# Two more tiles of u sent to DRAM, with the adding transfers of the last four tiles issued inside the down projection, and the first half's closing additions written to SBUF

## The chip, the cores and the metric

One Trainium2 chip, one core of it. The metric is the device time of one execution in microseconds, the median of three runs; lower is better. A profiled execution gives, beside its own time, a span: from the start of the first recorded instruction to the end of the last.

## The reference

One decoder layer over 256 tokens with 2048 channels: a normalised input projection, two kinds of attention, an output projection with a residual, and then the part that matters here:

```python
h = _rmsnorm(x, norm_mlp_pre[layer])
u = jnp.square(jax.nn.relu(h @ w_up[layer]))        # 256 x 8192
x = x + _rmsnorm(u @ w_down[layer], norm_mlp_post[layer])
```

Everything is float32, and the weights (w_up 2048 x 8192, w_down 8192 x 2048) come from DRAM once per run.

## The kernel before

**Split products.** Each float32 operand is split in two parts: `hi` is the value rounded by a ScalarE copy to the short format that TensorE takes at full speed, `lo = value - hi` is made by VectorE (L307, L308). A product is then three matmuls, hi.hi, lo.hi and hi.lo (`three`, `mm` at L297). So each weight tile of 128 x 1024 costs a load into a buffer `raw` on SP's DMA queue, a `hi` on ScalarE and a `lo` on VectorE, before TensorE uses it for twelve matmuls (two token blocks, two column halves, three parts). There are five `raw` buffers and eight `hi`/`lo` pairs; the class `Weights` makes the tiles six ahead of their use.

**Steps of seven products.** Some steps ("w" in the lists of steps) take two weight tiles and two column halves together by a scheme of seven products in place of eight (`seven_products`, L1055). Their two weight tiles are loaded as one pair of 1 MB on POOL's queue (L375), into one of two buffers in turn (`ab_down` and `c` in the first half of the down projection, `ab_down` and `u01` in the second). VectorE forms sums of them (L362, L366, L367), which are then split like other weights, and sums of the tokens' blocks (`four_sums`, L1011 to L1013), which are split into `s`. Three of the seven products go to banks of their own (`md`), and `close` (L1071) combines these into four tiles `c` in SBUF, which are added to the four accumulators at the end of the half.

**Up and down.** The up projection runs over eight column chunks j of 1024. Each is evacuated by `up_evac` (L934): ScalarE takes the relu into a buffer `r` (two of them), TensorE transposes it (L301), and ScalarE squares it into a tile of u. There are 16 such tiles g, each 128 x 1024 for 512 of the 8192 channels: chunk j gives tiles 2j and 2j + 1. The down projection has two halves c of 1024 output columns. Each half goes through all 16 tiles of u; a step takes 128 channels ("k") or 256 ("w"), so there are four k or two w to a tile. The steps of seven are those of `DOWN_SEVEN`: 5, 7, 9, 11, 15, 17, 19, 21, 25, 27, 29 in the first half (step kp uses tile kp // 2), and the odd ones from 3 to 27 in the second. The four accumulators `y` of the first half take four banks of PSUM, those of the second the other four; the second half's `md` take the banks of the first half's `y`.

**The parts of u.** In each half `split_u` makes uhi and ulo of the next tile while the present one is used. For tiles g in `AWAY` (4 to 11) ulo is not made by VectorE: after `up_evac`, `lo_away` (L954) lets ScalarE write the negated rounded tile into `r` (L961), stores that in DRAM (`ukeep`, L963, on ScalarE's queue), and later a transfer on POOL's queue adds u to it there (L968, `accum_op`), two halves of 256 KB each. What is then in DRAM is u - uhi. ulo is loaded back from it on POOL's queue (`load_lo`, L997) in both halves. For other tiles VectorE makes ulo in the first half, and `keep_u` (L1001, SP's queue) stores it for the second.

**What sets the order.** The instructions of each engine, and of each DMA queue, run in the order in which the program issues them. That order is made by a planner (`Flow`): side tasks are generators that yield planned microseconds, TensorE's instructions move the planned clock on (0.216 us a matmul), and after each group of matmuls `pump` lets every task whose time has come issue its next instructions. `until` and `finish` issue a task's instructions at once up to a point. `lo_away` yields 34 us (48 us for tiles 10 and 11) between the stores and the adding transfers. POOL's queue holds the pair loads, the u loads, the loads of kept sums (`skeep`) and the adding transfers. A transfer that waits for its buffer holds up all behind it on its queue.

**The first half's closing.** `half_evac` (L1207) runs as a task at the start of the second half. For each of the four accumulators VectorE adds `more` (the tile `c`) in PSUM (L1216), ScalarE squares the sum from PSUM and sums it over the row (L1164), and VectorE multiplies it by the gain into SBUF (L1211), one accumulator late. At the first step of seven of the second half (kp = 3, after six k steps) `flow.finish(h_evac)` (L1259) issues what is left of it before the banks become `md`.

Of the kernel before, what the change touches and what calls it, by code (L numbers as in the profile page):

```python
# [22 lines left out]
AF = mybir.ActivationFunctionType  # L23
OP = mybir.AluOpType
# [5 lines left out]
NB = S // P  # L30
# [84 lines left out]


DOWN_SEVEN = ((5, 7, 9, 11, 15, 17, 19, 21, 25, 27, 29), range(3, 28, 2))
AWAY = range(4, 12)
SHARED = [k for k in DOWN_SEVEN[0] if k in DOWN_SEVEN[1]]
GT = FF // 512  # L120
DOWN_STEPS = [[s for kp in range(2 * GT)
# [143 lines left out]
def layer(nc, tc, io):  # L265
# [688 lines left out]
    def lo_away(g):  # L954

        ukeep[g] = dram.tile([P, CW], F32, name=f"ukeep{g}")
        u = uT[g].rearrange("p k s -> p (k s)")
        for h in range(2):
            c = slice(h * 512, (h + 1) * 512)
            t = late["up"].tile([P, 512], F32, tag="r", bufs=2, name=f"neg{g}_{h}")  # L960
            nc.scalar.activation(t.bitcast(F32R), u[:, c], AF.Copy, scale=-1.0)  # L961
            yield 1.0
            nc.scalar.dma_start(out=ukeep[g][:, c], in_=t)  # L963
            yield 7.0
        yield 34.0 if g < 10 else 48.0
        for h in range(2):
            c = slice(h * 512, (h + 1) * 512)
            nc.gpsimd.dma_start(out=ukeep[g][:, c], in_=u[:, c], accum_op=OP.add)  # L968
            yield 2.0

    def split_u(c, g):
        if (c, g) == (0, 0):
# [186 lines left out]

        return uT[i + n // 2].rearrange("p k s -> p (k s)")[:, (n % 2) * 512:(n % 2) * 512 + 512]  # L1160

    def square(n, b):
        junk = dpl["dp"].tile([P, 512], BF16, tag="junk", bufs=1, name=f"junkd{n}{b}")
        nc.scalar.activation(junk, y[b][n], AF.Square, accum_out=ssd[b][:, n:n + 1])  # L1164

    def gain(n, b):
        yg[n, b] = spare(2 * b, n)
# [38 lines left out]

    def half_evac(more, g_half):  # L1207

        def half_gain(b, n):
            yg[n, b] = more[b, n]  # L1210
            nc.vector.tensor_tensor(out=more[b, n], in0=y[b][n], in1=g_half[n], op=OP.mult)  # L1211

        done = []
        for n in range(2):
            for b in range(NB):
                nc.vector.tensor_tensor(out=y[b][n], in0=y[b][n], in1=more[b, n], op=OP.add)  # L1216
                square(n, b)
                yield 1.0
                if done:
                    half_gain(*done.pop())  # L1220
                    yield 1.0
                done.append((b, n))
        half_gain(*done.pop())

    def three_more(out, a, w):

# [10 lines left out]
    for c in range(2):  # L1237

        for i, (b, n) in enumerate(PARTS):
            y[b][2 * c + n] = bank(4 * c + i, f"y{b}{2 * c + n}")  # L1240
        accs = {(b, n): y[b][2 * c + n] for b, n in PARTS}
        ws = DOWN_SEVEN[c]
        for t, (what, k, tiles) in enumerate(wide_d[c]):
            g = (2 * k if what == "w" else k) // 4
            u = us[c, g]
            if g >= GT - 2 and c:
                break
            if what == "k":
                w = weights.get(tiles[0])
                for b, n in PARTS:  # L1250
                    down_mm(c, u, k, b, n, w, t == 0, t == len(wide_d[c]) - 1)
                    flow.pump()
                weights.free(tiles[0])
            else:
                if k == ws[0]:
                    if not c:
                        flow.finish(*u_last)
                    else:
                        flow.finish(h_evac)  # L1259
                    m = {i: bank(4 * (1 - c) + o, f"md{i}_{c}") for o, i in enumerate((1, 6, 7, 5))}  # L1260
                blocks = [[tok(u[x], 2 * (k % 2) + kk, bb) for x in range(2)] for kk, bb in ((0, 0), (1, 0), (1, 1))]
                seven_products(tiles, (blocks, left.pop((c, k))), accs, m, k == ws[0], k == ws[-1])
                if k == ws[-1]:
                    more = close([spare(10, i) for i in range(4)] if c else closing(), m)
                if not c and k in SHARED:
                    keep_s(k)
            while c and loaded[0] < min(g + (2 if g > 2 else 1), GT - 1):
                loaded[0] += 1
                load_lo(c, loaded[0])
            nxt = (c, g + 1) if g < GT - 1 else (1, 0)  # L1270
            if nxt not in us:
                if not c and g > 1 and g - 1 not in AWAY:
                    keep_u(g - 1)
                us[nxt] = split_u(*nxt)
            if (c, what, k) == (0, "k", 3):
                weights.limit += 1
            if (c, what, k) == (0, "k", 36):
                g_half = [late["up"].tile([P, 512], F32, tag="r", bufs=2, name=f"g_half{n}") for n in range(2)]
                for n in range(2):
                    load_gain(n, g_half[n])  # L1280
            if (c, what, k) == (1, "k", 40):
                flow.start(x_back())
                for n in (2, 3):
                    load_gain(n, spare(4, n))
        if not c:
            keep_u(GT - 1)
            h_evac = flow.start(half_evac(more, g_half))
# [64 lines left out]
```

## Time and profile before

| | |
|---|---|
| median of 3 runs | 1050.45 us (1049.29 to 1050.63) |
| the profiled execution's own time | 1050.77 us |
| its span | 1049.0 us |
| TensorE busy | 1035.0 us (99%) |
| VectorE busy | 841.1 us (80%) |
| ScalarE busy | 639.5 us (61%) |
| POOL busy | 74.0 us (7%) |
| mean granted clock of TensorE | 0.997 |
| up projection, last chunk, first matmul of the down projection | from 659.2 us, 704.5 us |
| first and second half of the down projection meet at | about 873 us |

How the rows of a profile are read: a timeline row has the start, the duration, the engine (PE is TensorE, PEld its weight load, DVE VectorE, ACT ScalarE, SP and POOL the others; a q behind the name is the engine's queue), the line, the operation, what it writes and reads (out<-in), the shape and types, the count of merged instructions, and in brackets the idle time before it and what ended that. A row of waits has who waited for whom, the total, the count and the longest. A row of DMA issues has out<-in, the queue, the count, the size and the median time from issue to landing; a row of DMA queues has packets, MB and the time of its packets as a share of all 16 DMA engines. Matmuls overlap in the array: one is recorded with 0.39 us, and the next starts 0.227 us after it.

### The profile page before, as it was taken

To read this page: it belongs to the slowest core of one execution; us is meant where nothing else is said; L and a number is where in the kernel's file an instruction comes from. 1 tells how busy PE (TensorE), PEld (TensorE's weight loads), DVE (VectorE), ACT (ScalarE), POOL (GpSimd) and SP (SyncE) were. 2 spreads that over 40 slices of the span, in tenths; PEclk is the share of its full clock that TensorE was granted. 3 is DMA by queue.
4 is the path that set the end of the run, shared out by engine and by line. 5 is a ranking of instruction groups with operands and counts; after the bars stand their busy time and mean duration, and the time that the engine had idled before them with its cause. 6 is when DMAs were issued, how large, how long until landed. Compare 5 with 4: busy or idle time off the path is not lost.

```text
span 1049.0 us, 13419 instructions
## 1 busy us (share of the span) xinstructions
PE 1035.0 (99%) x4828; PEld 860.1 (82%) x4828; DVE 841.1 (80%) x1129; ACT 639.5 (61%) x870; POOL 74.0 (7%) x113
## 2 busy tenths in 40 slices
PE   9999999999999999999999999999999999999996
PEld 6888889888888788888888888788888888788885
DVE  6676536567557669999999999798989987998895
ACT  6584436565545466565766767666757564766561
POOL 0000000000000000000010102000101001112100
PEclk9999999999999999999999999999999999999998
DMA  9975447454447295646769769479696968789862
GB/s 299 357 236 153 139 133 238 145 162 157 145 160 240 82 369 188 208 155 213 234 201 299 191 221 265 154 263 342 207 379 224 356 213 290 264 307 352 331 232 81
DMA packets 85363, 240.87 MB, mean 230 GB/s; under 512 B 7472, under 2 KB 12080, under 8 KB 84912
## 3 DMA queue, kind: packets, MB, share of 16 engines
q1 hardware_dynamic: 62992, 165.70, 46.6%
q0 software_dynamic: 19568, 69.74, 20.3%
q10 hardware_dynamic: 2736, 4.57, 1.3%
q8 instruction: 38, 0.62, 0.2%
q14 instruction: 29, 0.24, 0.1%
HBM read 218.49 MB, written 21.50 MB: 229 GB/s over the span
## 4 chain that ended last, share of the span: by engine, by line
PE 87%; DVE 7%; issue 2%; DMA 2%; ACT 1%; SPq 0%; POOL 0%; DVEq 0%; POOLq 0%; ACTq 0%
PE acc_u L297 21%; PE y L297 20%; PE acc_o L297 8%; PE m L297 6%; PE md L297 5%; PE acc_v L297 4%; PE acc_qk L297 4%; DVE lo L308 3%; PE acc_ckv L297 2%; PE acc_ukv L297 2%; PE acc_q L297 2%; PE acc_cq L297 2%; PE acc_k L297 2%; PE acc_uq L297 2%; PE rt L301 1%
## 5 line engine op out<-in xcount | busy, mean ns | idle before, releaser
L308 DVE TENSOR_TENSOR lo<-raw,hi 128x1024 fp32r<-128x1024 f32 (+3 forms) x207 | 233.7, 1149 | 80.7 <-ACT hi L307 80.0
L307 ACT ACTIVATE hi<-raw 128x1024 fp32r<-128x1024 f32 (+3 forms) x207 | 203.6, 997 | 76.1 <-DMA raw<-in_w_in 15.3
L297 PE MATMUL acc_u<-hi,hT_hi 128*128 128x512 f32 x356 | 141.7, 398 | 0.0
L297 PE MATMUL acc_u<-hi,hT_lo 128*128 128x512 f32 x356 | 139.1, 391 | 0.4 <-DVE hT_lo L308 0.4
L297 PE MATMUL acc_u<-lo,hT_hi 128*128 128x512 f32 x356 | 138.7, 390 | 0.0
L297 PE MATMUL y<-lo,uhi 128*128 128x512 f32 x352 | 137.1, 389 | 1.0 <-DVE lo L308 1.0
L297 PE MATMUL y<-hi,uhi 128*128 128x512 f32 x352 | 137.3, 390 | 0.0
L297 PE MATMUL y<-hi,ulo 128*128 128x512 f32 x352 | 137.0, 389 | 0.0
L312 DVE SCALAR_TENSOR_TENSOR lo<-raw,gcol,hi 128x1024 fp32r<-128x1024 f32 x74 | 92.5, 1280 | 11.4 <-ACT hi L311 11.3
L311 ACT ACTIVATE hi<-raw,gcol 128x1024 fp32r<-128x1024 f32 x74 | 83.2, 1148 | 28.7 <-DMA raw<-in_w_up 16.0
L297 PEld LDWEIGHTS acc_u<-hi,hT_lo 128*128 128x128 f32 x356 | 66.8, 188 | 15.1 <-DVE hT_lo L308 0.9
L297 PEld LDWEIGHTS y<-lo,uhi 128*128 128x128 f32 x352 | 66.1, 188 | 15.0 <-DVE lo L308 1.4
L297 PEld LDWEIGHTS acc_u<-lo,hT_hi 128*128 128x128 f32 x356 | 67.0, 188 | 12.9
L297 PEld LDWEIGHTS y<-hi,ulo 128*128 128x128 f32 x352 | 66.1, 188 | 13.8
L297 PEld LDWEIGHTS acc_u<-hi,hT_hi 128*128 128x128 f32 x356 | 66.9, 188 | 12.7
L297 PEld LDWEIGHTS y<-hi,uhi 128*128 128x128 f32 x352 | 66.1, 188 | 13.6
L307 ACT ACTIVATE hi<-u 128x1024 fp32r<-128x1024 f32 (+1 forms) x38 | 37.4, 991 | 42.2 <-DVE u L367 30.1
L308 DVE TENSOR_TENSOR lo<-st_down,hi 128x1024 fp32r<-128x1024 f32 x48 | 57.6, 1220 | 4.2 <-ACT hi L307 4.2
L307 ACT ACTIVATE hi<-st_down 128x1024 fp32r<-128x1024 f32 x48 | 49.9, 1051 | 5.7 <-DVE st_down L367 3.2
L297 PE MATMUL md<-hi,s 128*128 128x512 f32 x144 | 52.2, 390 | 0.8 <-ACT uhi L980 0.8
L297 PE MATMUL acc_o<-hi,mixT_hi 128*128 128x512 f32 x128 | 51.8, 405 | 0.0
L297 PE MATMUL acc_o<-hi,mixT_lo 128*128 128x512 f32 x128 | 50.2, 392 | 0.0
(332 smaller groups left out, 2150.2 us busy)
## 6 DMA issues: line engine op xcount, KB each, us to landing
raw<-in_w_down SPq DMA_DIRECT2D x80, 512.0 KB, 5.8
raw<-in_w_up SPq DMA_DIRECT2D x76, 512.0 KB, 4.9
raw<-in_w_in SPq DMA_DIRECT2D x55, 512.0 KB, 5.0
ab<-in_w_up POOLq DMA_DIRECT2D x22, 1024.0 KB, 5.6
raw<-in_w_out SPq DMA_DIRECT2D x32, 512.0 KB, 4.3
ab_down<-in_w_down POOLq DMA_DIRECT2D x13, 1024.0 KB, 8.8
ulo<-ukeep POOLq DMA_DIRECT2D x23, 512.0 KB, 7.1
u<-in_w_down POOLq DMA_DIRECT2D x6, 1024.0 KB, 8.8
```

The source lines that it names most:

```text
L297: nc.tensor.matmul(out, a, b, start=start, stop=stop)
L301: nc.tensor.transpose(out, a, ident)
L307: nc.scalar.activation(hi, src, AF.Copy)
L308: nc.vector.tensor_tensor(out=lo, in0=src, in1=hi.bitcast(F32), op=OP.subtract)
L311: nc.scalar.activation(hi, src, AF.Copy, scale=g)
L312: nc.vector.scalar_tensor_tensor(out=lo, in0=src, scalar=g, in1=hi.bitcast(F32), op0=OP.mult, op1=OP.subtract)
```

## The change

Three things, all after the sixth up chunk:

- `AWAY` grows by the tiles 12 and 13. Each of them now has its negated rounded tile stored from ScalarE during the last up chunk, its u added in DRAM, and its ulo loaded on POOL's queue in the first half. VectorE's subtraction for it in the first half and the store of its ulo on SP go.
- For tiles 10 to 13 (`g >= LATE`) the adding transfers wait, in the planner, for the start of the down projection (`dpl` filled), and are then issued 4, 9, 24 and 29 planned us later, the second half of a tile 10 planned us after the first. Before, those of 10 and 11 were issued 48 planned us after their stores.
- `half_evac` first adds all four accumulators and `more` into SBUF (into `more` itself), which frees the banks; 20 planned us later it squares and multiplies each from SBUF, one each 5 planned us. The second half's `md` banks are taken when the four additions are issued (`added`), not when the whole task is.

```diff
-AWAY = range(4, 12)
+AWAY = range(4, 14)
+LATE = 10
...
@@ lo_away
-        yield 34.0 if g < 10 else 48.0
+        if g < LATE:
+            yield 34.0
+        else:
+            while not dpl:
+                yield 2.0
+            yield 4.0 + 5.0 * (g % 2) + 20.0 * ((g - LATE) // 2)
         for h in range(2):
             c = slice(h * 512, (h + 1) * 512)
             nc.gpsimd.dma_start(out=ukeep[g][:, c], in_=u[:, c], accum_op=OP.add)
-            yield 2.0
+            yield 2.0 if g < LATE else 10.0
...
-    def square(n, b):
+    def square(n, b, of=None):
         junk = dpl["dp"].tile([P, 512], BF16, tag="junk", bufs=1, name=f"junkd{n}{b}")
-        nc.scalar.activation(junk, y[b][n], AF.Square, accum_out=ssd[b][:, n:n + 1])
+        nc.scalar.activation(junk, y[b][n] if of is None else of, AF.Square, accum_out=ssd[b][:, n:n + 1])
...
     def half_evac(more, g_half):
 
-        def half_gain(b, n):
+        order = [(b, n) for n in range(2) for b in range(NB)]
+        for b, n in order:
             yg[n, b] = more[b, n]
-            nc.vector.tensor_tensor(out=more[b, n], in0=y[b][n], in1=g_half[n], op=OP.mult)
-
-        done = []
-        for n in range(2):
-            for b in range(NB):
-                nc.vector.tensor_tensor(out=y[b][n], in0=y[b][n], in1=more[b, n], op=OP.add)
-                square(n, b)
-                yield 1.0
-                if done:
-                    half_gain(*done.pop())
-                    yield 1.0
-                done.append((b, n))
-        half_gain(*done.pop())
+            nc.vector.tensor_tensor(out=yg[n, b], in0=y[b][n], in1=yg[n, b], op=OP.add)
+        added[0] = True
+        yield 20.0
+        for b, n in order:
+            square(n, b, yg[n, b])
+            yield 4.0
+            nc.vector.tensor_tensor(out=yg[n, b], in0=yg[n, b], in1=g_half[n], op=OP.mult)
+            yield 1.0
+
+    added = [False]
...
                     if not c:
                         flow.finish(*u_last)
                     else:
-                        flow.finish(h_evac)
+                        flow.until(lambda: added[0])
```

## The prediction

> **What bounds the kernel now.** I read the page first (busy shares), then the waits of TensorE, then the stretches in which it waits, then the queues that the change touches.
>
> ```profile
> span 1049.0 us, 13419 instructions
> PE 1035.0 (99%) x4828; PEld 860.1 (82%) x4828; DVE 841.1 (80%) x1129; ACT 639.5 (61%) x870; POOL 74.0 (7%) x113
> ...
> PE rt L301 <- ACT r L938: 1.4, 1, 1.4
> PE y L297 <- DVE lo L308: 1.0, 1, 1.0
> PE md L297 <- ACT uhi L980: 0.8, 1, 0.8
> ```
>
> TensorE is idle for 14.0 of 1049.0 us. The three rows are all of its waits after 600 us, 3.2 us together. The change touches nothing that runs earlier and adds or removes no matmul; the closing tail of the second half stays as it is. So 3.2 us is the most it can win, and the question is which waits go and whether new ones come.
>
> The first wait, in the chain of waits (start, length), with one row of VectorE's timeline:
>
> ```profile
> 651.61 8.49 DMA raw<-in_w_up
> ...
> 662.60 2.49 DVE acc_u L1143 x4
> ...
> 670.72 0.66 PE rt L301 x4
> ...
> 661.39 1.28 DVE L312 SCALAR_TENSOR_TENSOR lo<-raw,gcol,hi 128x1024 fp32r<-128x1024 f32 x1 [2.36 <-ACT hi L311]
> ```
>
> A weight tile asked for at 651.61 takes 8.49 us to land. VectorE stands idle for 2.36 us before its part of the split; its additions of 662.60, the relu and the transposes follow, 1.4 us late. What loads the DMA then is in POOL's timeline, in a DMA view of 646 to 662 us and in the table by stretches (columns: stretch, length, busy time of PE, PEld, DVE, ACT, POOL, clock, DMA share, GB/s):
>
> ```profile
> 648.42 0.74 POOL L375 DMA_DIRECT2D ab<-in_w_up  x1 [12.14 <-DVE lo L308]
> 649.15 3.53 POOL L968 DMA_DIRECT2D ukeep<-ab  x4
> ...
> q0 software_dynamic: 806, 2.04, 57.8%
> ...
> raw<-in_w_up SPq DMA_DIRECT2D x2, 512.0 KB, 5.2
> ...
> 646.00:668.00 22.00, 22.00 (x101) 17.98 (x101) 19.37 (x23) 11.42 (x14) 4.26 (x5) 1.00 0.98 312
> 668.00:680.00 12.00, 10.60 (x51) 8.53 (x50) 8.99 (x11) 10.50 (x13) 0.00 (x0) 1.00 0.00 0
> ```
>
> Right ahead of that tile POOL issues the four adding transfers of u tiles 10 and 11. The DMA is full until 668 and then empty; two like tiles asked for at 681 land in 5.2 us.
>
> The other two waits lie in the first half's closing additions (timelines of VectorE, ScalarE and TensorE; the third row is VectorE's waits from 880 to 892 us: total, times, longest):
>
> ```profile
> 877.18 0.69 DVE L308 TENSOR_TENSOR lo<-ab_down,hi 128x512 fp32r<-128x512 f32 x1
> 877.78 1.29 DVE L1216 TENSOR_TENSOR y<-y,c 128x512 f32<-128x512 f32 x2
> DVE lo L308 <- ACT hi L307: 6.3, 3, 2.8
> ...
> 891.38 1.28 DVE L1211 TENSOR_TENSOR c<-y,g_half 128x512 f32<-128x512 f32 x2
> ...
> 895.16 2.35 DVE L308 TENSOR_TENSOR lo<-raw,hi 128x1024 fp32r<-128x1024 f32 x2
> ...
> 884.37 0.60 ACT L1164 ACTIVATE junkd<-y 128x512 bf16<-128x512 f32 x1 [2.56 <-DVE y L1216]
> ...
> 892.21 0.47 PE L297 MATMUL md<-hi,s 128*128 128x512 f32 x1 [0.81 <-ACT uhi L980]
> ...
> 896.43 0.50 PE L297 MATMUL y<-lo,uhi 128*128 128x512 f32 x1 [1.00 <-DVE lo L308]
> ```
>
> The two engines wait in turn: a square on ScalarE waits for an addition on VectorE, the hi split stands behind the square, the lo split waits for it, and the next addition stands behind that. VectorE loses 6.3 us in three such waits, and at 895.16 it makes a tile that TensorE already wants. The row at 892.21 names uhi, but that matmul reads hi and s only; what it writes is a bank of the first half, and the two multiplications that free the last banks start at 891.38, 0.64 us each. I take it as a wait for the first of them.
>
> **The change part by part.**
>
> (1) The transfers of u10 and u11 leave 649 us: up to 1.4 us. Without them the tile should land in 5.2 us, 3.3 earlier, and VectorE's idle 2.36 us go; that is more than the 1.4 us by which the transposes are late. If the planner's clock puts the first of the four before the first pair load (4 to 6 planned us against about 5.6), POOL, which runs ahead, still issues that one at 649: a quarter of the load stays, and 2.5 us are won at the tile, still enough. Bounds: 0 and 1.4; I take 1.4.
>
> (2) Eight adding transfers enter the down projection. Their cost on the DMA: queue q0's 57.8% of 16 us is 9.25 us for 2.04 MB; over the whole run it is
>
> ```profile
> q0 software_dynamic: 19568, 69.74, 20.3%
> ...
> 705.00:735.00 30.00, 30.00 (x141) 24.82 (x140) 25.89 (x33) 19.93 (x26) 2.02 (x3) 1.00 0.92 327
> 735.00:745.00 10.00, 10.00 (x45) 8.28 (x45) 8.65 (x11) 6.76 (x9) 1.25 (x2) 1.00 0.59 177
> 745.00:760.00 15.00, 15.00 (x68) 12.39 (x67) 14.83 (x19) 11.44 (x13) 1.81 (x3) 1.00 0.62 225
> ```
>
> 213 us for 69.74 MB, of which 16 x 0.26 = 4.2 MB are added. Two equations give 2.85 us per MB for a plain load and 6.3 for an adding one, so 1.65 us of all 16 engines for each transfer of 0.26 MB and 13.2 for eight. Free capacity is 2.4 us up to 735, 4.1 up to 745 and 5.7 up to 760: together 12.2. It nearly fits, but some 7 us late around 745. Who could miss it there is the pair of step 11, in these rows of POOL, VectorE and TensorE:
>
> ```profile
> 704.82 0.74 POOL L375 DMA_DIRECT2D ab_down<-in_w_down  x1 [52.14 <-DVE acc_u L1143]
> ...
> 737.34 0.56 POOL L997 DMA_DIRECT2D ulo<-ukeep  x1 [14.84 <-PE y L297]
> 737.89 0.70 POOL L375 DMA_DIRECT2D c<-in_w_down  x1
> ...
> 751.94 1.23 DVE L362 TENSOR_TENSOR st_down<-c 128x1024 f32<-128x1024 f32 x1
> ...
> 754.54 2.35 DVE L308 TENSOR_TENSOR lo<-raw,hi 128x1024 fp32r<-128x1024 f32 x2
> ...
> 758.63 0.39 PE L297 MATMUL y<-hi,uhi 128*128 128x512 f32 x1
> ```
>
> By the planned times the transfers of u10 and u11 come after the first pair load (704.82), the first halves of u12 and u13 before the third, the second halves between 737.34 and 737.89. Each holds POOL for 3.53 / 4 = 0.9 us, covered by idle time like the 14.84 us at 737.34, so that only the load of 737.89 starts later, by 1.8 us. VectorE reads that pair at 751.94. Its tile of 754.54 is done at 755.7 and wanted at 758.86, one matmul after the last row: 3.1 us to spare, so the pair may land as late as 755.0. From 704.82 to it q0 must carry three pairs (9.0 us of all engines), eight additions (13.2), one u load (1.5) and this pair (3.0): 26.7 us. At the 57.8% share that q0 had in the crowded stretch that takes 46.2 us, to 751.0. I count nothing; if the cover is gone, see the rivals. The raw tiles on SP share the engines: with 7 us of delay and the same 3.1 us to spare, 3.9 at most; nothing taken, as they are asked for up to five tiles ahead.
>
> (3) u12 and u13 are stored negated. Added: four ScalarE copies of a square's width (0.60 at 884.37) and four DMA issues, all after the transposes of 672 us, where the DMA is empty. Nearest to the edge is the tile at 678.49:
>
> ```profile
> 678.49 2.48 DVE L312 SCALAR_TENSOR_TENSOR lo<-raw,gcol,hi 128x1024 fp32r<-128x1024 f32 x2
> ...
> 681.23 0.39 PE L297 MATMUL acc_u<-hi,hT_hi 128*128 128x512 f32 x1
> ```
>
> It is done at 679.8, wanted at 681.46. One or two copies ahead of it (0.6 or 1.2 us) still fit in 1.7; none counted, bounds 0 and 1. Removed in the first half: two lo subtractions on VectorE (1.2 each, as at 895.16) and two stores on SP, which held up its raw loads. Added: two u loads on POOL, which wait until TensorE is done with tiles 10 and 11.
>
> ```profile
> ab_down<-in_w_down POOLq DMA_DIRECT2D x13, 1024.0 KB, 8.8
> ...
> c<-in_w_down POOLq DMA_DIRECT2D x1, 1024.0 KB, 14.5
> ...
> 809.41 0.53 POOL L997 DMA_DIRECT2D ulo<-ukeep  x1 [9.65 <-PE y L297]
> ...
> 810.64 0.72 POOL L375 DMA_DIRECT2D c<-in_w_down  x1
> ...
> 832.06 1.23 DVE L362 TENSOR_TENSOR st_down<-c 128x1024 f32<-128x1024 f32 x1
> ```
>
> The pair of 810.64 stands behind the new load, which is released one u tile (9.65 + 0.53 us) after 809.41, and starts at 820.2. In the median time of its kind, 8.8 us (first row), it lands at 829, before it is read at 832.06; in the 14.5 us that it took here, beside another pair just ahead, at 834.7, 2.6 late, of which the subtraction of u13 behind it gives 1.2 back. Bounds 0 and 1.4; nothing, since the pair ahead then has ten us to itself. The next pair stands behind the load of tile 13 in the same way.
>
> (4) The closing. Four additions in a row (4 x 0.65) free the four banks at about 880.4 instead of 892. VectorE saves 6.3 us of waiting ahead of 895.16 and four multiplications (2.6), 8.9 in all against 1.0 of wait. Both waits go: 1.8 us. The multiplications and the squares (4 x 0.6 on ScalarE) come back 20 to 40 planned us later, one each 5 us; the 8.9 us cover them. Without that cover they would cost up to 2.6. Reading SBUF in place of PSUM is priced at nothing: two additions in PSUM take 1.29 us, one lo split of the same width in SBUF 0.69.
>
> The sum: 1049.0 - 1.4 - 1.8 = 1045.8 of span; the profiled execution took 1050.77, 1.77 more than its span, so 1047.6; it lies 0.32 above the median of 1050.45. **Forecast: 1047.3 us.**
>
> **The rivals.**
>
> Slower: q0 falls behind. The 26.7 us that q0 must carry reach the pair of step 11 at 704.8 + 26.7 / share. At a share below 0.53 the pair lands after 755.0 and TensorE waits; below 0.48 the wait is over 5.3 us and the kernel slower by over 0.2%. At 0.46 it lands at 762.8, costs 7.8 us and gives 1055.1. For it: 92% load at 705 to 735, and VectorE busy for 14.83 of 15 us from 745, with nothing to catch up in. Against it: the 57.8% seen with the same transfers.
>
> Half share: with exactly half of the engines the pair lands at 758.2, 3.2 us too late, and the time is 1050.5. The Trainium skill (DMA: Bandwidth & Descriptors, Queues, rings and completion order) says that a DMA engine takes turns between the queues that have work, and works off one queue's descriptors in order; by that rule two busy queues get half each and the pair stands behind the additions. The 57.8% differ from it a little to the good. The Trainium skill (Collectives: The Full Stack, The bandwidth ceiling) also puts an addition at two source reads, twice a plain transfer; the trace agrees, with 6.3 against 2.85 us per MB.
>
> Half effect: the relu's wait stays, because pair and weight tiles fill the DMA at 649 without the additions too: 1.4 us less won, 1048.7. For: 0.98 load; against: the tiles that land in 5.2.
>
> The change doesn't do what it says: the tile of 895.16 is late for its raw or pair data and not for VectorE, the bank for the split of s. Then 1.4 is all, and with a lost 1 us under (3) it is 1050.0. Against: between 877 and 896 no row waits for a DMA.
>
> **How the numbers follow.** Forecast 0.52 (its own range 1046.5 to 1048.3); half effect 0.17; half share 0.11; not as it says 0.08; slower 0.12. 0.2% of 1050.45 is 2.1 us, about what can be told from no change: faster means below 1048.35. That is the forecast and four tenths of the half effect, 0.59; slower 0.12; the rest, 0.29, no change. The range takes in all but the slow case, and reaches down by the spread of the runs: 1046.4 to 1050.9.
>
> **What would show it.** No wait of TensorE at rt and none in 885 to 900; the tile of 651.6 landing before 658; y + c four times in a row, into SBUF. Against it: a wait for DVE lo between 745 and 765, with VectorE waiting for c or ab_down just before; a wait near 681; a raw tile late at 705 to 725. The forecast falls if any of these costs over 1 us.

## The result and the profile after

The changed kernel takes 1046.45 us, the median of 7 runs (1046.13 to 1048.6), beside 1050.01 us of the kernel before in the same comparison (1049.29 to 1050.63): ratio 0.9967, with a 95% interval of 0.9956 to 0.9978. That is 3.6 us less, 2.3 to 4.6 by the interval, where 3.2 were forecast. The profiled execution took 1046.13 us.

The page of the kernel after, with the lines that answer to those of before (in the chain that ended last PE now has 97%, DVE 1%; before PE 87%, DVE 7%):

```profile
span 1044.4 us, 13426 instructions
PE 1034.1 (99%) x4828; PEld 860.1 (82%) x4828; DVE 839.3 (80%) x1127; ACT 641.2 (61%) x874; POOL 78.6 (8%) x119
```

All of TensorE's waits after (engine, line, what released it: total, times, longest):

```profile
PE warm L523 <- DVE zero L520: 1.2, 1, 1.2
PE acc_u L298 <- DVE hT_lo L309: 0.4, 1, 0.4
PE acc_qk L298 <- ACT hi L308: 0.2, 1, 0.2
PE qrt L302 <- DVE qT L774: 0.2, 1, 0.2
```

The rows rt (1.4), y (1.0) and md (0.8) are gone, and no recorded wait has come in their place: the last one left starts at 367 us. Where the relu's weight tile was late before, the view of raw's instructions from 650 to 652 us now has its issue and landing:

```profile
L192 SPq DMA_DIRECT2D raw<-in_w_up x1: 327/327/327, 651.0 to 651.0; - x1
...
DMA to landing us min/median/max: 5.1/5.1/5.1
```

and the table by stretches reads:

```profile
646.00:668.00 22.00, 22.00 (x103) 18.20 (x102) 21.31 (x24) 13.37 (x17) 1.63 (x2) 1.00 0.76 263
668.00:680.00 12.00, 12.00 (x58) 9.94 (x57) 8.22 (x10) 9.86 (x13) 0.00 (x0) 1.00 0.15 32
```

The tile lands in 5.1 us instead of 8.49, the DMA is busy for 76% of the stretch instead of 98%, and TensorE is busy for all of both stretches. POOL's timeline shows where the adding transfers went:

```profile
648.56 0.90 POOL L974 DMA_DIRECT2D ukeep<-ab  x1
...
702.47 0.73 POOL L376 DMA_DIRECT2D ab_down<-in_w_down  x1 [53.00 <-PE acc_u L298]
703.20 2.67 POOL L974 DMA_DIRECT2D ukeep<-ab  x3
705.67 0.93 POOL L376 DMA_DIRECT2D c<-in_w_down  x1
706.40 1.98 POOL L974 DMA_DIRECT2D ukeep<-ab  x2
...
735.77 1.82 POOL L974 DMA_DIRECT2D ukeep<-ab  x2
736.89 1.44 POOL L376 DMA_DIRECT2D c<-in_w_down  x1
```

DMA views show what POOL's queue carried from 702.4 to 749.8 us (packets, MB, share of 16 engines), and how long the pair issued at 736.89 took to land (last number):

```profile
q0 software_dynamic: 2290, 6.76, 48.9%
...
c<-in_w_down POOLq DMA_DIRECT2D x1, 1024.0 KB, 12.8
```

One of the eight is still issued at 649, as POOL runs ahead to the first pair load; seven lie between the pairs. VectorE's timeline at the two pairs and in the closing:

```profile
724.98 1.23 DVE L363 TENSOR_TENSOR st_down<-c 128x1024 f32<-128x1024 f32 x1 [0.85 <-DMA c<-in_w_down]
...
749.81 1.23 DVE L363 TENSOR_TENSOR st_down<-c 128x1024 f32<-128x1024 f32 x1
...
875.68 2.48 DVE L1218 TENSOR_TENSOR c<-y,c 128x512 f32<-128x512 f32 x4
...
884.19 2.35 DVE L309 TENSOR_TENSOR lo<-raw,hi 128x1024 fp32r<-128x1024 f32 x2
```

VectorE waits 0.85 us for the pair of 705.67 and nothing measurable for that of 736.89: it landed at 749.7, just ahead of the row of 749.81 that reads it. The four additions are one row, and the weight tile that was made at 895.16 before is made at 884.19.

Waits alone don't say how much each part is worth. All kernels here issue the same 4828 matmuls in the same order, so I number them by start and subtract the start in before from the start in the other kernel; what a stretch adds to that difference is what it won (minus) or lost. The rows below belong to the kernels of the experiments; the first stretch, up to 658 us, lies ahead of the change.

```
                                up to 658   658-705    705-800   800-885   885-end    all
                                 (start)   (rt wait)  (pairs)             (closing)
after                             -0.58      -1.77      +0.22      0.00     -2.39    -4.52
closing only                      +0.35      +0.26       0.00      0.00     -2.39    -1.78
transfers only                    +0.91      -1.77      +0.30      0.00     -0.13    -0.69
no u12, u13                       +0.76      -1.77      -0.02      0.00     -2.39    -3.42
u10, u11 early                    -0.34      +0.10      +0.52      0.00     -2.38    -2.10
interleaved, to SBUF              +1.25      -1.79      +0.24      0.00     -0.10    -0.40
no delay                          -0.08      -1.79      +0.20      0.00     -2.38    -4.05
additions in the banks            -0.85      -1.77      +0.13      0.00     -2.39    -4.88
in the banks, no u12, u13         -0.44      -1.79      -0.02      0.00     -2.38    -4.63
plain writes                      -0.21      -1.76      +0.32      0.00     -1.73    -3.38
copy only                         +3.59      -1.77       0.00      0.00     -2.39    -0.57
three more transfers              +3.37      -1.76      +3.71      0.00     -2.38    +2.94
seven more transfers              +2.98      -1.79      +9.27      0.00     -2.38    +8.08
```

The profiled spans differ by 4.6 us, but 0.58 of that lies ahead of the change, in the first 20 us, which differ by up to 2 us between the executions of the table (-0.85 to +1.25, the three with the copy left out). The change itself won 3.94 in this trace: 1.77 at the transposes and 2.39 at the closing, less 0.22.

### The profile page after: what moved, and what is told of

Read it like the earlier page. It is cut to its first block, busy times and chain, and to the rows that moved or that the text cites. A ratio compares the mean times of both kernels' runs of the same rounds, so it can differ in the third digit from the quotient of the medians.

```text
span 1044.4 us, 13426 instructions
## 1 busy us (share of the span) xinstructions
PE 1034.1 (99%) x4828; PEld 860.1 (82%) x4828; DVE 839.3 (80%) x1127; ACT 641.2 (61%) x874; POOL 78.6 (8%) x119
## 3 DMA queue, kind: packets, MB, share of 16 engines
q1 hardware_dynamic: 62704, 164.66, 46.2%
## 4 chain that ended last, share of the span: by engine, by line
PE 97%; DVE 1%; issue 1%; DMA 0%; ACT 0%; POOL 0%; SPq 0%; DVEq 0%; POOLq 0%; ACTq 0%
PE y L298 24%; PE acc_u L298 24%; PE acc_o L298 8%; PE m L298 7%; PE md L298 6%; PE acc_qk L298 4%; PE acc_v L298 4%; PE acc_ckv L298 2%; PE acc_ukv L298 2%; PE acc_q L298 2%; PE acc_cq L298 2%; PE acc_k L298 2%; PE acc_uq L298 2%; PE rt L302 1%; PE sc_b L298 1%
```

## The experiments

The experiments separate the parts (four kernels), look into the closing (three) and into the transfers (four), and end with a smaller version. The medians of before beside them lie between 1050.02 and 1050.49 us.

**The closing alone.** Before with the new `half_evac`, `square` and the step that waits for `added`; `AWAY` and the transfers as before.

```
-        flow.finish(h_evac)
+        flow.until(lambda: added[0])
         (and half_evac as in the change)
```

> Before with the new closing alone (the additions to SBUF, the squares and factors later; u10 to u13 are handled as before). Theory: the two closing waits (0.81 and 1.00 recorded) go and the wait at the transposes near 670 us (1.40) stays; by starts of TensorE's tiles in the trace of after the closing is worth 2.4, so about 1047.6 (1050.0 - 2.4), TensorE without an idle gap between 880 and 910 us. Rival A: it is worth the recorded idle only, 1.8: 1048.2. Rival B: TensorE waited for late additions and not for the squares' reads of the banks, so the second of the two waits stays: about 1049.

Measured: 1048.14 us beside 1050.49, ratio 0.998 (0.9971 to 0.9989), 2.35 us less. Of TensorE's waits after 600 us one row is left:

```profile
PE rt L301 <- ACT r L938: 1.6, 2, 1.4
```

Both closing waits are gone and rt stays, as the theory has it. The size is 2.39 us by the starts, not the 1.8 of recorded idle, and the medians' 2.35 agree. The 1047.6 that was expected started from 1050.0; beside it before took 1050.49 this time.

**The transfers alone.** After with the closing of before.

```
-        flow.until(lambda: added[0])
+        flow.finish(h_evac)
         (and half_evac as before the change)
```

> After with the closing of before (additions in the banks, square and factor between them); the adding transfers of u10 to u13 as in after. Theory: the transposes' wait near 670 us goes (1.76 by the starts of the tiles, 1.40 recorded), the closing's two waits of 0.81 and 1.00 stay: about 1048.2 (1050.0 - 1.8). With the closing alone this sums to the whole, 3.6 to 4.2. Rival: the eight adding transfers in the down projection cost something that the new closing hides (its later squares leave the u loads free): 1049 or more, and gaps on TensorE between 700 and 830 us.

Measured: 1049.08 us beside 1050.49, ratio 0.999 (0.9981 to 0.9999), 1.4 us less. Its waits:

```profile
PE y L298 <- DVE lo L309: 1.0, 1, 1.0
...
PE md L298 <- ACT uhi L986: 0.7, 1, 0.7
```

The rt row is gone and the closing's two stay. The two kernels together, 2.35 and 1.4, make 3.8 beside the 3.6 of the whole change: the parts add up, as independent parts would. By the time alone the rival (1049 or more) would fit too; the table sets it at 0.30 lost between 705 and 800 us, and that loss is in after as well, so the new closing doesn't hide it.

**Without u12 and u13.**

```
-AWAY = range(4, 14)
+AWAY = range(4, 12)
```

> After with u12 and u13 split by VectorE as before (no stores, no adding transfers, no loads for them); u10 and u11 and the closing stay as in after. Theory: u12 and u13 are worth nothing either way, VectorE having slack there: 1046.5, within 0.4. Rival A: their four adding transfers cost some of the pair loads' time: faster, about 1046.0. Rival B: VectorE's two splits (2.6 each) were late for something between 780 and 850 us: slower, 1047 to 1048, with a TensorE gap at the first tiles of u12 or u13.

Measured: 1046.47 us beside 1050.49, ratio 0.9965 (0.9951 to 0.9978), as after. The 0.22 us of the table go with u12 and u13. In after, TensorE's second transposes of u15 start right behind the relu (ScalarE and TensorE, timelines of after):

```profile
708.72 0.67 ACT L939 ACTIVATE r<-acc_u,rstd_pre 128x512 f32<-128x512 f32 x1
...
709.44 0.66 PE L302 MATMUL rt<-ident,r 128*128 128x128 f32 x4
```

and in the kernel without u12 and u13 there are 0.94 us between them (709.02 + 0.67 = 709.69, against 710.63):

```profile
709.02 0.67 ACT L939 ACTIVATE r<-acc_u,rstd_pre 128x512 f32<-128x512 f32 x1
...
710.63 0.60 PE L302 MATMUL rt<-ident,r 128*128 128x128 f32 x4
```

So the part for u12 and u13 won nothing and cost about 0.2 us there. No row of waits shows it, as the matmul record ahead of these transposes overlaps them. ScalarE's timeline of after has what holds the relu up:

```profile
686.33 1.58 ACT L308 ACTIVATE hi<-raw_w 128x512 fp32r<-128x512 f32 x2 [0.48 <-ACT neg L962]
...
707.23 0.63 ACT L308 ACTIVATE s<-st_down 128x512 fp32r<-128x512 f32 x1 [1.81 <-DVE st_down L1019]
```

The relu of 708.72 stands behind a split that waits 1.81 us for VectorE's sums (1.39 in the kernel without u12 and u13). VectorE is late because ScalarE makes its hi splits later: the copies of the negated tiles now stand ahead of them, as in the row of 686.33. Counted against the matmuls, that relu comes 1.04 us later in after than in before. In the kernels of the table without these copies it isn't late and nothing is lost. In seven that have them it is 0.94 to 1.34 us late and 0.13 to 0.52 are lost, with the copy alone 0.83 and nothing: the loss is the lateness less about 0.8 us each time.

**u10 and u11 early.** After with their transfers where before has them.

```
-LATE = 10
+LATE = 12
...
         if g < LATE:
-            yield 34.0
+            yield 34.0 if g < 10 else 48.0
```

> After with the adding transfers of u10 and u11 back where before has them (at about 649 us by the planner's clock, ahead of the raw tile's load); u12, u13 and the closing stay as in after. Theory: the raw tile lands late again and the wait at the transposes near 670 us returns, 1.40 recorded and 1.76 by the starts: 1048.2. Rival: the wait of before came from chance in that execution or from the stores alone: 1046.5, no gap.

Measured: 1048.76 us beside 1050.49, ratio 0.9984 (0.9975 to 0.9993). The wait is back:

```profile
PE rt L302 <- ACT r L939: 1.7, 2, 1.4
```

It costs 1.87 us by the table (+0.10 against -1.77). The kernel before, the one with the closing alone and this one have it, the eleven with late transfers don't. So the transfers of u10 and u11 ahead of the weight tile make that wait; chance and the stores alone are out.

**Interleaved, but to SBUF.** After with the additions to SBUF, in the order and spacing of before.

```
+        for n in range(2):
+            for b in range(NB):
+                yg[n, b] = more[b, n]
+                nc.vector.tensor_tensor(out=yg[n, b], in0=y[b][n], in1=yg[n, b], op=OP.add)
+                square(n, b, yg[n, b])
...
+                yield 1.0
+                if done:
+                    half_gain(*done.pop())     # yg * g_half, in place
+                    yield 1.0
...
-        flow.until(lambda: added[0])
+        flow.finish(h_evac)
```

> After with the closing additions to SBUF, but each followed at once by its square and the factor of the one before, in the order and spacing of before, and the step of md waiting for all of them as before. Forecast's reading: the two closing waits have two causes, the first (md, 0.8) the banks still to be read by squares and factors, the second (y, 1.0) VectorE's lateness from waiting for squares. The banks are free after the last addition at about 888 us, so the first wait goes, VectorE still waits some 6 us for ScalarE and the second stays: about 1048.0, half of the closing's 2.4 won against the kernel with the transfers alone (1049.1). Rival: both waits are the one lateness of VectorE; freed of the first, TensorE waits the whole 1.8 to 2.4 at the second: 1049.1, nothing won. Rival 2: reading from SBUF is enough, both go: 1046.7.

Measured: 1050.23 us beside 1050.13, ratio 0.9999 (0.9988 to 1.0009). Its twelve runs spread over 5 us (1047.79 to 1052.79), the widest of all kernels here, which was not explained, so the reading rests on its trace. There 1.25 us are lost ahead of the change, and from 658 us to the end it won 1.65, as the transfers alone did (1.60). VectorE's waits from 872 to 892 us:

```profile
DVE lo L309 <- ACT hi L308: 6.4, 3, 2.8
```

and TensorE's waits:

```profile
PE y L298 <- DVE lo L309: 2.0, 1, 2.0
```

This is the first rival: the md wait is gone, so it was a wait for a bank, but the y wait has grown from 1.0 to 2.0. The tile that TensorE waits for is made at 894.76 in this kernel, which is 895.05 in before's time (895.16 before), and TensorE only reaches it earlier. Freeing the banks by itself is worth nothing.

**Without the delay.** After with squares and factors right behind the four additions.

```
         added[0] = True
-        yield 20.0
+        yield 1.0
         for b, n in order:
             square(n, b, yg[n, b])
-            yield 4.0
+            yield 1.0
```

> After with the 20 us ahead of the squares and factors cut to 1 and the 4 us between square and factor to 1, so that they come right behind the four additions. Theory: the additions in one go are what frees the banks; the weight tile at 884 us has 6.6 us of slack, and factors (2.6) and a few waits for squares eat it without a stall: 1046.5, no TensorE gap. Rival: VectorE's factors wait for squares that stand behind hi splits on ScalarE, 2 to 3 us each as before, 6 us or more, and the gap at 896 us returns: 1047.5 to 1048.5.

Measured: 1046.76 us beside 1050.13, ratio 0.996 (0.9949 to 0.9972), no TensorE wait in the closing. VectorE's timeline at the weight tile:

```profile
888.15 1.22 DVE L309 TENSOR_TENSOR lo<-raw,hi 128x1024 fp32r<-128x1024 f32 x1
```

Three of the factors now come ahead of the tile (the first at 880.18), which is made at 888.15, 4 us later than in after (3.5 with the starts of the two kernels aligned), and still in time. The delay wins nothing here.

**Additions in the banks, in one go.** After with `y[b][n]` as the additions' output, squares and factors reading the banks right behind.

```
+        for b, n in order:
+            nc.vector.tensor_tensor(out=y[b][n], in0=y[b][n], in1=more[b, n], op=OP.add)
+        yield 1.0
+        for b, n in order:
+            square(n, b)
+            yg[n, b] = more[b, n]
+            nc.vector.tensor_tensor(out=yg[n, b], in0=y[b][n], in1=g_half[n], op=OP.mult)
+            yield 1.0
...
-        flow.until(lambda: added[0])
+        flow.finish(h_evac)
```

> After with the four closing additions in one go but in the banks, as before has them, squares and factors right behind and reading the banks; the step of md waits for all of it. Theory after the interleaved run (VectorE's lateness alone makes both waits): the additions in one go no longer make ScalarE and VectorE wait in turn, the factors (2.6) fit in the 6.6 us of slack, the banks are free before 888 us: 1046.7, no TensorE gap; the move to SBUF is then not needed. Rival: the banks matter by themselves: squares on ScalarE stand behind hi splits that wait for TensorE, the banks come free after 891 us and the md wait of 0.8 or more stays: 1047.5 to 1049.

Measured: 1046.29 us beside 1050.05, ratio 0.9966 (0.9952 to 0.9979); the closing wins the same 2.39. VectorE's timeline:

```profile
874.19 2.49 DVE L1217 TENSOR_TENSOR y<-y,c 128x512 f32<-128x512 f32 x4
...
886.33 2.35 DVE L309 TENSOR_TENSOR lo<-raw,hi 128x1024 fp32r<-128x1024 f32 x2
```

and its waits for a hi split from 872 to 892 us:

```profile
DVE lo L309 <- ACT hi L308: 0.3, 1, 0.3
```

Four additions in a row end the waiting in turn (0.3 us instead of 6.3), and nothing else of the new closing is needed: neither SBUF nor the delay. The multiplications are done by 881.7, so the banks are free in time as well.

**Three and seven more adding transfers.** After with further adding transfers of the same size, right behind the named ones, into a tile that nothing reads; a third kernel has only the first added line below, the copy that fills that tile.

```
+        nc.sync.dma_start(out=scr[b], in_=xs[b])        # where xkeep[b] is written
...
             nc.gpsimd.dma_start(out=ukeep[g][:, c], in_=u[:, c], accum_op=OP.add)
+            if g in (LATE, LATE + 1) and (g, h) != (LATE, 0):      # seven: g >= LATE and (g, h) != (LATE, 0)
+                o = (g - LATE) % 2 * CW + h * 512
+                nc.gpsimd.dma_start(out=scr[(g - LATE) // 2][:, o:o + 512], in_=u[:, c], accum_op=OP.add)
```

> After with three more adding transfers only, behind the second of u10's and both of u11's, all issued between 703 and 708 us. Theory: the c load of 705.7 lands 8 us later (733, VectorE reads it at 725, the next weight tile has 7.5 of slack), the ab load of 720.6 lands at 743 (read at 739.2, slack behind it 3.1 to 3.5): stalls of 0.5 to 3, 1047 to 1049.5. Rival: absorbed, 1046.5 and no gap; then the margin in after is more than three transfers.

> After with seven more adding transfers of the same size, one right behind each of the eight but the first, into a tile that nothing reads (filled by a copy at about 350 us); output as before. Theory of the slower rival (transfers ahead of the pair loads delay them): after's adding transfers land 2.7 us apart while weights load, so the c load of 705.7 lands 8 us later (733), the ab load of 720.6 some 13 later (748 against its reading at 739.2), the c load of 736.9 some 10 later (760 against 752.9, its reading at 749.8 and 3.1 of slack): stalls of 7 to 12 in sum, 1053 to 1059. Rival: the DMA engines absorb them, q0's weights being first: under 1047.5.

> After with only the copy that fills the unread tile of the two runs with more transfers (2 MB at about 350 us), and no more transfers. In those two runs TensorE lost 2.4 to 2.6 us at 368 and 414 us, ahead of all of this. Theory: that is the copy's doing, so 1048.9 here, and the three transfers cost 3.7 of the 6.1 us, the seven 10.2 of 12.6. Rival: the loss belongs to those runs, 1046.5 here.

Measured for the three: with three more 1052.52 us (ratio 1.0017, 1.0007 to 1.0026), seven more 1059.03 (1.008, 1.0063 to 1.0098), the copy alone 1049.79 (0.9994, 0.9985 to 1.0003). The times forecast for the first two, 1047 to 1049.5 and 1053 to 1059, were both passed, as they left out the copy. It costs 3.3 us over after by itself, where 2.4 were expected. In its trace 1.7 are lost at 368 us, where TensorE waits 1.33 and 0.48 us (before only 0.42), and 1.55 behind it, where the granted clock is 0.50 for 3.4 us and matmuls start 0.427 us apart instead of 0.227. The table by stretches has:

```profile
369.50:372.80 3.30, 3.30 (x11) 2.68 (x10) 1.14 (x3) 0.60 (x1) 0.00 (x0) 0.50 0.68 278
```

The kernel with three more has the two waits too (1.29 and 0.49 us), but not the lower clock.

Against the copy alone three more transfers cost 2.7 us and seven 9.2. The stalls forecast were 0.5 to 3 and 7 to 12, so the theory holds for both, and the margin in after is less than three transfers. The table has 3.7 and 9.3 between 705 and 800 us, and not all of that is theirs. Of the 3.7, 1.39 are lost at u15's transposes, whose relu is 2.21 us late; VectorE was late by as much at its additions of 707.73, when the first of the further transfers was only being issued (707.72). That leaves 2.3 for them. What made VectorE late there was not followed further. In the kernel with three more, POOL's timeline has:

```profile
706.42 0.74 POOL L376 DMA_DIRECT2D ab_down<-in_w_down  x1 [52.98 <-PE acc_u L298]
...
710.80 2.42 POOL L376 DMA_DIRECT2D c<-in_w_down  x1
717.77 0.86 POOL L976 DMA_DIRECT2D ukeep<-ab  x1 [4.55 <-DMA ab_down<-in_w_down]
```

and VectorE's waits from 705 to 775 us:

```profile
DVE st_down L363 <- DMA c<-in_w_down: 8.6, 1, 8.6
DVE st_down L363 <- DMA ab_down<-in_w_down: 1.2, 1, 1.2
```

VectorE waits 8.6 us for the pair issued at 710.80, which is step 7's; the pair of step 11, on which the forecast's slower rival rested, isn't among its waits. In the kernel with seven more the waits go on to step 11. Its waits of TensorE:

```profile
PE y L298 <- DVE lo L309: 5.4, 3, 4.2
```

and of VectorE from 705 to 775 us:

```profile
DVE st_down L363 <- DMA c<-in_w_down: 12.8, 2, 8.8
```

Right behind the longest of TensorE's waits, 4.2 us, the granted clock is 0.50 for 3.4 us here too, which makes 1.7 of the 9.3 us:

```profile
767.60:771.00 3.40, 3.40 (x8) 2.75 (x9) 3.40 (x4) 3.40 (x4) 0.00 (x0) 0.50 0.69 239
```

**Plain writes.** After with the eight transfers of u10 to u13 not adding. This kernel leaves the addition out for them: what it loads back as ulo of these four tiles is u itself, in both halves of the down projection.

```
-            nc.gpsimd.dma_start(out=ukeep[g][:, c], in_=u[:, c], accum_op=OP.add)
+            nc.gpsimd.dma_start(out=ukeep[g][:, c], in_=u[:, c],
+                                **({} if g >= LATE else {'accum_op': OP.add}))
```

> After with the eight transfers of u10 to u13 as plain writes: the addition is left out, so the low halves of u10 to u13 in the second half are u itself and the output is not the reference's. Theory: an addition of 0.26 MB takes 1.65 us of all 16 engines and a plain write 0.75, so with 58% of the engines the c load of 705.7, three transfers ahead of it, lands 4.7 us earlier (724.9 to 720) and that of 736.9, two ahead, 3.1 earlier (749.7 to 746.6); the time stays, 1046.5, since those pairs had slack. Rival: what delays the pairs is the number of transfers in the queue, not that they add: both land within 1 us of after.

Measured: 1046.96 us beside 1050.05, ratio 0.997 (0.9959 to 0.9981). DMA views from 702.8 to 748.3 us (q0), and of the two pair loads, issued at 737.32 and at 706.13:

```profile
q0 software_dynamic: 1792, 6.55, 40.4%
...
c<-in_w_down POOLq DMA_DIRECT2D x1, 1024.0 KB, 10.9
...
c<-in_w_down POOLq DMA_DIRECT2D x1, 1024.0 KB, 16.7
```

The pairs land in 16.7 and 10.9 us instead of 19.2 and 12.8, so 2.5 and 1.9 us sooner: more than the rival's 1, less than the 4.7 and 3.1 of the theory. Up to the landing of step 11's pair q0 took 0.404 x 45.5 = 18.4 us of all engines here and 0.489 x 47.4 = 23.2 in after. The 0.21 MB by which after's stretch holds more are 0.6 of that (at 18.4 / 6.55 = 2.8 us per MB). Seven additions thus cost 4.2 us more than seven plain writes, 0.6 each, where the forecast had 1.65 - 0.75 = 0.9. By this estimate an adding transfer is 1.35 us, 1.8 times a plain one. The time stays, so at this number of transfers their adding is covered; the 0.66 that this kernel lost after 885 us in the table is a wait at 985, far from these transfers, and was not followed.

**A smaller version.** The additions in one go in the banks, and no u12 and u13.

```
 (as in the banks, and)
-AWAY = range(4, 14)
+AWAY = range(4, 12)
```

> The smaller version that the runs point to: additions in one go in the banks, squares and factors right behind, u10 and u11 added late, u12 and u13 split by VectorE as before. Theory: by the starts of TensorE's tiles after wins 3.96 over before from 20 us on, the kernel without u12 and u13 4.30 and the one with the additions in the banks 4.06; together 4.3 to 4.4, so about 1046.1 against 1046.45 of after, no idle gap of TensorE after 370 us. Rival: without the u12 and u13 part the four splits on VectorE (2.6 more in 810 to 830 us) or the earlier factors leave a gap, 1046.7 or more.

Measured: 1047.02 us beside 1050.02, ratio 0.9971 (0.9961 to 0.9982). From 658 us on it wins 4.19 us by the table, against 3.94 in after, with no wait there, but by the time it can't be told from after; the 1046.1 that was expected was not reached. It is simpler, not faster.

## Why the prediction was right, step by step

**Which waits bound the kernel.** Right in the main: the three waits after 600 us went, and after 367 us no wait is recorded. But "3.2 us is the most it can win" was a misreading: by the starts the change won 4.16 us. A matmul is recorded with 0.389 us, and the next one starts 0.227 us after it. So idle time counted from the end of a record leaves out 0.16 us, and behind the matmuls of 892.21 and 896.43, recorded with 0.47 and 0.50, the next start is another 0.08 and 0.11 later. By the starts, then, the two closing waits cost 2.39 instead of 1.81, and the wait of the transposes of 670.72 cost 1.6 instead of 1.40. The other 0.16 of the 1.77 were lost at the transposes of 664.07, which wait for a relu as well but start before the record ahead of them ends, so that no idle time shows it. What after loses at 709.44 is hidden in the same way.

**(1) The transfers leave 649 us.** Right in mechanism, as u10 and u11 early shows; the tile landed at 656.1, before the 658 that was asked for. One transfer did stay at 649, as step (1) allowed. The term was mis-sized, as just said: 1.4 against 1.77.

**(2) Eight adding transfers in the down projection: nothing.** Right in the sum, and by two errors that met. For the pair of step 11 the forecast had 26.7 us of all engines at a share of 57.8%, 46.2 us. (Its two equations give 6.1 us per MB for an addition, not 6.3, which takes 0.4 off the 26.7.) Measured are 23.2 us at 48.9%, 47.4 us, after an issue of the first pair at 702.47, 2.35 earlier than before, as TensorE was ahead by that. It landed at 749.7, which is 751.8 in before's time, against 751.0. The additions were cheaper than priced (0.6 above a plain write, not 0.9; one of the eight lay elsewhere), and q0's share was no constant. DMA views of after from 712 to 720, 720 to 730 and 730 to 735 us, and of the kernel with three more from 740 to 746:

```profile
q0 software_dynamic: 462, 1.04, 56.3%
q1 hardware_dynamic: 412, 1.50, 49.3%
...
q0 software_dynamic: 557, 1.56, 53.7%
q1 hardware_dynamic: 558, 2.02, 51.7%
...
q1 hardware_dynamic: 387, 1.41, 69.5%
q0 software_dynamic: 179, 0.67, 32.6%
```

```profile
q0 software_dynamic: 560, 1.72, 98.7%
q1 hardware_dynamic: 23, 0.07, 3.3%
```

With additions waiting on q0 and weights on q1 the two take about as much each; with a single pair in flight q0 takes a third, and with q1 nearly empty almost all. The Trainium skill (DMA: Bandwidth & Descriptors, Queues, rings and completion order) has a DMA engine take turns between the queues that have work, and the first of these shares agrees with it. The forecast had set half shares aside for its 57.8%. The half-share rival had the better share, then, and failed because there was less to carry. The Trainium skill (Collectives: The Full Stack, The bandwidth ceiling) puts an addition at twice a plain transfer, and the 1.8 measured here agrees with that better than the forecast's own 2.2. What step (2) missed is the pair of step 7: it stands behind three additions, VectorE already waits 0.85 us for it in after, and it is the first to be late when more is queued. POOL's cost per issue was set too high: the first three of 703.20 start 0.55 us apart (703.20, 703.76, 704.30), and step 11's load was issued at 736.89 + 2.13 = 739.0 in before's time, 1.1 later and not 1.8.

**(3) u12 and u13: nothing.** Right within its bounds of 0 and 1; measured is a loss of about 0.2 us, at u15's transposes and not at the tile of 678 us or the pair of 810. The step counted the ScalarE copies, and at the tile of 678 us, half a microsecond late by them in after's trace, their delay fits as it said. It did not follow the delay on to the relus of u15, where VectorE is 1.0 us late and some 0.8 are to spare.

**(4) The closing: 1.8.** The result was right, mis-sized at 2.39. Of its two reasons one carried the gain. VectorE's waiting in turn was the cause; four additions in a row remove it, and the tile of 895.16 was in time: 884.19 is 886.3 in before's time, 8.8 us earlier, where the forecast had 8.9. The banks were a true wait, as read from the md row, but no gain of their own: freed alone, they hand their 0.8 us to the next wait. With the additions in a row they are free in time anyway, so the move to SBUF could have been left out, and so could the delay of the squares: in the two kernels that do without it, about 3.5 and 2.5 us of the time won came back on VectorE ahead of the tile (starts aligned) and cost nothing.

**The sum.** 3.2 forecast, 3.94 in the trace from 658 us on, 3.56 by the medians. The profiled executions of before and after differ by 4.64, 0.58 of which is the start. The error of the sum is in the size of its two terms.

**The rivals.** Half effect: out, the wait at rt is gone. Not as it says: out, VectorE's lateness was it. Half share and slower: not in this kernel, but their mechanism is real. Three more transfers of 0.26 MB turn the gain into a loss against the copy alone of 2.7 us, seven 9.2, so the chance of 0.23 for these two was not idle. The place was wrong: step 7's pair first, not step 11's.

## What to carry to other kernels

Work out what a wait is worth from the starts of the instructions on both sides, not from the recorded idle time, and ask where the next instruction would wait if this one didn't: one of two waits in a row can be worth nothing alone. When two engines wait for each other in turn, issuing one engine's whole batch first removed nearly all of it here; where the results went didn't matter. A queue that takes extra transfers for nothing can be less than three transfers from its limit, so look at each load behind them and not only at the last one.

## What the runs showed of the hardware

A wait of TensorE with 0.8 to 1.4 us of recorded idle time cost 0.2 to 0.3 us more than that. An adding transfer of 0.26 MB from SBUF to DRAM cost about 1.35 us of all 16 engines, an estimate, 0.6 above a plain write; the five issued between 703 and 707 us, beside weight loads, took 11 to 23 us from issue to landing. The ninth transfer on POOL's queue was not issued until the first of the eight ahead of it had landed: in the kernel with three more, the one of 717.77 waited 4.55 us for the ab_down load of 706.42, with seven others between. That limit is the program's: in the trace these transfers raise eight semaphores in turn, and the instruction of 717.77 itself waits for the one that the load raised last at 717.48.

An additional copy of 2 MB, in two transfers issued at 357 and 370 us, cost TensorE 1.7 us through its waits at 368 us and, in the profiled execution, 1.55 more through 3.4 us at a granted clock of 0.50 right behind them. The same 3.4 us at 0.50 followed a wait of 4.2 us in the kernel with seven more transfers. They followed neither the same two waits in the kernel with three more nor the wait of 1.4 in before.
